# MLP with block products by seven in a hybrid decoder layer: operand sums moved to VectorE, splits spread over the group, weight sums issued earlier, last group as eight plain products

## The chip, the core and the metric

The kernel runs on one core of a Trainium2 chip. Its engines are TensorE (PE, matrix products, with PEld for loading the stationary operand), VectorE (DVE), ScalarE (ACT), GpSimd (POOL) and SyncE (SP, which only issues DMAs). Each engine works through its own queue in order; they wait for each other through semaphores. The metric is device time in microseconds (us), the median of several runs. The span of a profile is the time from its first to its last instruction; the time of that execution is a little longer.

## The reference

One decoder layer over 512 positions, width 1024, in float32: two attention branches merged by gates, an output projection, then an MLP with hidden width 4096 and squared ReLU, and a last RMSNorm. The change touches the MLP and the last norm alone:

```
h2 = rmsnorm(x, mlp_norm_g[l])
x = x + jnp.square(jax.nn.relu(h2 @ w_ff1[l])) @ w_ff2[l]
...
return rmsnorm(x, final_norm_g)
```

## The kernel before

Float32 products are made of three float32r products: each operand is split into a high part (ACT copies it to float32r, `hi`) and a low part (DVE subtracts, `lo`), and `mm3` adds hi·hi, hi·lo and lo·hi in PSUM. A matmul has a stationary operand of 128x128 and up to 512 columns.

The MLP runs over 8 groups of 512 hidden channels. For a group, four ff1 blocks (`ff1`, called a, b, c, d here; 24 matmuls each) give z = relu(.)², held as z0 and z1 (two blocks of 128 channels each, 512 tokens). The product of z (512 tokens by 512 channels) with 512 rows of w_ff2 (by 1024 columns) is then made as a 2x2 block product with seven instead of eight block multiplications (Winograd's form of Strassen's algorithm). Its operands (`ORDER`) are A11, A12, A22 (blocks of z), the sums S1 to S4 of blocks of z, B11, B21, B22 (blocks of w_ff2) and the sums T1 to T4 of blocks of w_ff2. A product k is a `pair` of two units (m = 0, 1), six matmuls of 512 columns each, 12 together, into PSUM tiles `pl` (four of them). Its result goes into `acc`, the residual of 512x1024, or into the running sums U (products 0 and 3) and V (product 2), all by DVE (L987 to L995).

- The sums S (`operand_a`) are POOL operations on 128x512; `put_a` then splits an A operand (ACT L959, DVE L960).
- `raw` loads a B block (512 KB, SP, L921). `tsum` makes a T: SP loads one block (L926) and POOL issues an accumulating DMA that adds the other (L927, from w_ff2 or from another T). There are three buffers for B blocks, three for T. `put_b` splits a B operand (ACT L967, DVE L968) into one of five buffers.
- The weights of ff1 come through `pre` (SP L112, ACT L119, DVE L121), two blocks ahead.
- `ff1` evicts its PSUM tile by ACT: relu (L911), then square (L912).

In group g the order is 0 a 1 2 b 3 4 c 5 d 6: digits are the products of group g, letters the ff1 blocks of group g+1. The order on PE is that of the code. On the other engines a scheduler sets the order when the program is built. Before, S1, S2, S4 and S3 of the next group and the splits of its operands 1 to 5 stand together behind block d. The last group has no ff1 blocks; it does the products 0 and 1, then 2 to 6 for m = 0 and for m = 1, and `finish` folds U and V into `acc` between them; `final` makes the last norm and stores rows of the result.

Of the kernel before, what the change touches and what calls it, by code (L numbers as in the profile page):

```python
# [10 lines left out]
F32 = mybir.dt.float32  # L11
F32R = mybir.dt.float32r
# [37 lines left out]
def body(nc, tc, ctx, a, out, dbg=lambda name, ap: None):  # L50
# [880 lines left out]
    def load(g, i):  # L931
        if g < NG:
            f, key = LOADS[i]
            f(g, key)

    def operand_a(g, key):
        z0, z1 = Z.get((g, 0)), Z.get((g, 1))
        t0, t1 = slice(0, 256), slice(256, 512)
        if key[0] == "A":
            return (z0, z1)[int(key[2]) - 1][:, :, (t0, t1)[int(key[1]) - 1]]  # L940
        if (g, key) not in SS:
            t = SS[g, key] = z_p.tile([128, 2, 256], F32, tag="s", name=key, bufs=3)
            if key == "S1":
                pool.tensor_tensor(t, z0[:, :, t1], z1[:, :, t1], op=ALU.subtract)
            elif key == "S2":
                pool.tensor_tensor(t, operand_a(g, "S1"), z0[:, :, t0], op=ALU.subtract)
            elif key == "S3":
                pool.tensor_tensor(t, z0[:, :, t0], z0[:, :, t1], op=ALU.subtract)
            else:
                pool.tensor_tensor(t, z1[:, :, t0], operand_a(g, "S2"), op=ALU.add)  # L950
        return SS[g, key]

    def put_a(g, k):
        if k % 2 == 0:
# [6 lines left out]
        AS[g, "op", k] = (hi, lo)  # L961

    def put_b(g, k):
        key = ORDER[k][1]
# [8 lines left out]
    def unit(g, k, m, cuts=(0, 512)):  # L973
        p = pl_tile()
        ah, al = AS[g, "op", k]
        bh, bl = BS[g, k]
        ms = slice(m * 128, (m + 1) * 128)
        for lo, hi in zip(cuts, cuts[1:]):
            c = slice(lo, hi)
            mm3(p[:, c], [(ah[:, q, ms], al[:, q, ms], bh[:, q, c], bl[:, q, c]) for q in range(2)])  # L980
            i, n = BLOCK.get(k, (0, 0))
            b = 2 * i + m
            cs = slice(512 * n + lo, 512 * n + hi)
            if k in BLOCK:
                t = acc[:, b, cs]
                if k == 5:
                    dve.tensor_tensor(t, t, p[:, c], op=ALU.subtract)  # L987
                else:
                    dve.tensor_tensor(t, p[:, c], t, op=ALU.add)  # L989
            t = {0: U, 2: V, 3: U}.get(k)  # L990
            if t is not None:
                if g == 0 and k != 3:
                    act.activation(t[:, m], p, AF.Copy)
                else:
                    dve.tensor_tensor(t[:, m], p[:, c], t[:, m], op=ALU.add)  # L995
            if g == NG - 1:
                finish(k, m, b, n, cs)

    def finish(k, m, b, n, cs):
        c12, c21, c22 = acc[:, m, 512:], acc[:, 2 + m, :512], acc[:, 2 + m, 512:]  # L1000
        if k == 3:
            pool.tensor_tensor(c21, c21, U[:, m], op=ALU.add)
            pool.tensor_tensor(V[:, m], U[:, m], V[:, m], op=ALU.subtract)
            pool.tensor_tensor(c12, c12, V[:, m], op=ALU.subtract)
        elif k == 5:
            pool.tensor_tensor(c21, c21, c22, op=ALU.subtract)
            dve.tensor_tensor(c22, c22, V[:, m], op=ALU.subtract)
        if k in (1, 4, 5, 6):
            final(b, n, cs)

    def pair(g, k):
        for m in range(2):
            unit(g, k, m)
        n = NP * g + k + NBS
        if n < NP * NG:
            put_b(*divmod(n, NP))

    def group(g):
        for step in "0a1 2b3 4c5 d6 ":
            if step.isdigit():  # L1020
                pair(g, int(step))
                load(g + 1, int(step))
            elif step != " ":
                ff1(4 * (g + 1) + "abcd".index(step))
            if step == "b":
                put_a(g + 1, 0)
            if step == "d":
                for k in range(1, 6):
                    put_a(g + 1, k)
        put_a(g + 1, 6)  # L1030

    def last_group(g):
        for k in range(2):
            pair(g, k)
        for m in range(2):
            for k in range(2, NP):
                unit(g, k, m, (0, 256, 512) if m and k == NP - 1 else (0, 512))
# [54 lines left out]
    for k in range(NP):  # L1092
        put_a(0, k)
        if k < NBS:
            put_b(0, k)
# [8 lines left out]
    last_group(NG - 1)  # L1104
    ff_st.close()
    right.close()

# [44 lines left out]
```

## Time and profile before

| | |
|---|---|
| median of the runs | 762.25 us |
| lowest | 758.26 us |
| the profiled execution | 762.06 us, span 760.3 us |
| PE busy | 701.6 us (92%) |
| DVE, ACT, POOL busy | 520.7, 366.1, 252.8 us (68%, 48%, 33%) |
| granted TensorE clock, mean | 0.963 of full speed |

Busy shares are means over stages with different limits; the group loop of the MLP runs from about 386 us to the end. The granted clock has two levels, full (2.4 GHz) and half (1.2 GHz); a mean between them in a stretch says that both occurred.

### The profile page before, as it was taken

Reading aid. Unit: us, or ns where it says so; the run is one execution under the profiler, and the core shown is the slowest. Engines: PE = TensorE matmul, PEld = TensorE weight load, DVE = VectorE, ACT = ScalarE, POOL = GpSimd, SP = SyncE. Lnnn points to the kernel's source line nnn. Section 1 sums busy time; section 2 is a strip of 40 time slices with the busy share of each in tenths; the row PEclk is TensorE's granted clock in tenths of the full one; section 3 lists DMA queues with packets and bytes.
Section 4 is the critical chain, followed back from the end, with each engine's and each line's share of the span. In section 5 each row is a group of like instructions: output and inputs, shape, how many; then the busy total and the mean of one; then the engine's idle time right before and its main releaser. Section 6 shows DMA issues by size and latency. Waiting matters only on the chain.

```text
span 760.3 us, 10231 instructions
## 1 busy us (share of the span) xinstructions
PE 701.6 (92%) x3653; PEld 563.8 (74%) x3654; DVE 520.7 (68%) x920; ACT 366.1 (48%) x631; POOL 252.8 (33%) x275
## 2 busy tenths in 40 slices
PE   8999999999999999999975989989899897999962
PEld 7879787778657778888954877868788686877852
DVE  6587899999998646833337558385664947557483
ACT  6566866646444456511426444344534534444333
POOL 2323677742365413200214141130413104141265
PEclk9999999999999999999996999989999998999996
DMA  8532521122311178800486956658476584644303
GB/s 316 194 119 81 159 87 43 56 70 87 109 42 44 56 273 318 254 27 1 154 238 178 254 145 185 175 139 210 122 212 176 140 214 131 180 111 108 87 1 110
DMA packets 43235, 106.55 MB, mean 140 GB/s; under 512 B 4464, under 2 KB 5360, under 8 KB 43184
## 3 DMA queue, kind: packets, MB, share of 16 engines
q1 hardware_dynamic: 35664, 88.04, 34.7%
q0 software_dynamic: 6656, 16.78, 12.7%
q10 hardware_dynamic: 864, 1.08, 0.4%
q8 instruction: 29, 0.48, 0.3%
q14 instruction: 22, 0.18, 0.1%
HBM read 90.28 MB, written 6.29 MB: 127 GB/s over the span
## 4 chain that ended last, share of the span: by engine, by line
PE 50%; DVE 18%; DMA 17%; POOL 5%; ACT 5%; issue 4%; SPq 0%; POOLq 0%; DVEq 0%; ACTq 0%
DMA T<-wff 8%; DMA T<-T 7%; PE pl L141 6%; PE pl L143 6%; PE pl L142 6%; PE pl L237 3%; PE pl L238 3%; PE pl L239 3%; DVE b L968 3%; PE pt L141 2%; PE pt L142 2%; PE pt L143 2%; DVE nmx L590 2%; DVE oh L714 2%; DVE as L960 2%
## 5 line engine op out<-in xcount | busy, mean ns | idle before, releaser
L141 PE MATMUL pl<-b,as 128*128 128x512 f32 (+1 forms) x226 | 94.7, 419 | 42.5 <-ACT z L911 18.2
L121 DVE TENSOR_TENSOR wlo<-wraw,whi 128x1024 fp32r<-128x1024 f32 (+1 forms) x60 | 73.8, 1231 | 68.5 <-ACT whi L119 67.7
L119 ACT ACTIVATE whi<-wraw 128x1024 fp32r<-128x1024 f32 (+1 forms) x71 | 74.5, 1049 | 87.5 <-PE pt L142 69.7
L143 PE MATMUL pl<-b,as 128*128 128x512 f32 (+1 forms) x226 | 93.2, 412 | 1.9 <-DVE as L960 1.9
L142 PE MATMUL pl<-b,as 128*128 128x512 f32 (+1 forms) x226 | 93.2, 412 | 0.0
L141 PE MATMUL pt<-h2h,whi 128*128 128x512 f32 x232 | 90.3, 389 | 0.0
L142 PE MATMUL pt<-h2l,whi 128*128 128x512 f32 x232 | 90.3, 389 | 0.0
L143 PE MATMUL pt<-h2h,wlo 128*128 128x512 f32 x232 | 90.3, 389 | 0.0
L141 PEld LDWEIGHTS pl<-b,as 128*128 128x128 f32 x226 | 46.0, 203 | 56.0 <-ACT z L911 20.6
L927 POOL DMA_DIRECT2D T<-wff x16 | 19.6, 1239 | 129.5 <-DMA T<-wff 60.8
L927 POOL DMA_DIRECT2D T<-T x16 | 14.1, 880 | 129.2 <-DMA T<-wff 60.3
L968 DVE TENSOR_TENSOR b<-T,b 128x1024 fp32r<-128x1024 f32 x32 | 39.7, 1240 | 24.6 <-ACT b L967 24.6
L143 PEld LDWEIGHTS pl<-b,as 128*128 128x128 f32 x226 | 46.0, 203 | 12.6 <-DVE as L960 2.7
L960 DVE TENSOR_TENSOR as<-S,as 128x512 fp32r<-128x512 f32 x32 | 33.4, 1081 | 29.7 <-ACT as L959 29.5
L142 PEld LDWEIGHTS pl<-b,as 128*128 128x128 f32 x226 | 46.1, 204 | 9.5
L967 ACT ACTIVATE b<-T 128x1024 fp32r<-128x1024 f32 x32 | 33.6, 1052 | 37.7 <-DMA T<-T 15.6
L141 PEld LDWEIGHTS pt<-h2h,whi 128*128 128x128 f32 x232 | 43.8, 189 | 9.2
L142 PEld LDWEIGHTS pt<-h2l,whi 128*128 128x128 f32 x232 | 43.6, 188 | 9.2
L143 PEld LDWEIGHTS pt<-h2h,wlo 128*128 128x128 f32 x232 | 43.6, 188 | 9.1
L714 DVE TENSOR_SCALAR oh<-posbc,thr 128x400 bf16<-128x400 f32 (+31 forms) x128 | 45.7, 410 | 3.8 <-PE pl L735 3.6
L989 DVE TENSOR_TENSOR acc<-pl,acc 128x512 f32<-128x512 f32 (+1 forms) x65 | 42.4, 671 | 7.8 <-PE pl L143 4.5
L595 POOL TENSOR_SCALAR pra<-pra,rs 128x400 f32<-128x400 f32 (+31 forms) x32 | 35.2, 1110 | 35.1 <-DVE rs L594 35.0
(315 smaller groups left out, 1730.6 us busy)
## 6 DMA issues: line engine op xcount, KB each, us to landing
wraw<-wff SPq DMA_DIRECT2D x32, 512.0 KB, 4.5
T<-wff SPq DMA_DIRECT2D x32, 512.0 KB, 4.5
wraw<-wF SPq DMA_DIRECT2D x24, 512.0 KB, 3.3
B<-wff SPq DMA_DIRECT2D x24, 512.0 KB, 6.4
T<-wff POOLq DMA_DIRECT2D x16, 512.0 KB, 7.6
T<-T POOLq DMA_DIRECT2D x16, 512.0 KB, 5.0
gd<-gt SPq DMA_DIRECT2D x16, 256.0 KB, 2.2
wraw<-wbr SPq DMA_DIRECT2D x8, 512.0 KB, 4.4
```

The lines of the kernel that those rows point to most:

```text
L119: act.activation(hi, raw, AF.Copy)
L121: eng.tensor_tensor(lo, raw, hi.bitcast(F32), op=ALU.subtract)
L141: pe.matmul(ps, lh, rh, start=(i == 0), stop=False)
L142: pe.matmul(ps, lh, rl, start=False, stop=False)
L143: pe.matmul(ps, ll, rh, start=False, stop=(i == n - 1))
L595: pool.tensor_scalar(pr, pr, rs, None, op0=ALU.mult)
L714: dve.tensor_scalar(oh[:, :n], posbc[:, :n], thr[:, 4 * G + q:4 * G + q + 1], None, op0=ALU.is_le)
L927: pool.dma_start(t, TT[g, y] if y[0] == "T" else wsrc(g, y), accum_op=ALU.add)
L960: dve.tensor_tensor(lo, x, hi.bitcast(F32), op=ALU.subtract)
L967: act.activation(t[:, 0], x, AF.Copy)
L968: dve.tensor_tensor(t[:, 1], x, t[:, 0].bitcast(F32), op=ALU.subtract)
L989: dve.tensor_tensor(t, p[:, c], t, op=ALU.add)
```

## The change

The operand sums S1 to S4 become DVE operations, in a function `asum`, and are issued at given places of the group. S1 and S2 of the next group come after block d, S3 and the split of A12 after product 6; the splits of products 2 to 6 come in their own group (after products 0, 1, 2 and so on). The T sums T1, T3, T2 of the next group are all issued after product 1, T4 after product 4; the B splits keep their places but go through a list `bq`. The last group is made of eight plain block products: its two halves of z are split whole (`last_put`, 128x1024), U and V are folded into `acc` before it (`last_sums`), and each block of 128x512 of the result gets 12 matmuls, one eviction and `final`. PE's order in groups 0 to 6 doesn't change.

```
-    LOADS = ((raw, "B11"), (raw, "B21"), (tsum, "T1"), (tsum, "T3"), (tsum, "T2"), (raw, "B22"), (tsum, "T4"))
...
+    def asum(g, key):
+        z0, z1 = Z[g, 0], Z[g, 1]
+        t0, t1 = slice(0, 256), slice(256, 512)
+        x, y, op = {"S1": (z0[:, :, t1], z1[:, :, t1], ALU.subtract),
+                    "S2": (SS.get((g, "S1")), z0[:, :, t0], ALU.subtract),
+                    "S3": (z0[:, :, t0], z0[:, :, t1], ALU.subtract),
+                    "S4": (z1[:, :, t0], SS.get((g, "S2")), ALU.add)}[key]
+        t = SS[g, key] = z_p.tile([128, 2, 256], F32, tag="s", name=key, bufs=3)
+        dve.tensor_tensor(t, x, y, op=op)
...
-                pool.tensor_tensor(t, z0[:, :, t1], z1[:, :, t1], op=ALU.subtract)
...
-            if g == NG - 1:
-                finish(k, m, b, n, cs)
...
+    LASTB = ("B11", "B21", "B12", "B22")
+
+    def last_put(j):
+        t = utile(j, F32R, "al")
+        hi, lo = t[:, 0:2], t[:, 2:4]
+        act.activation(hi, Z[NG - 1, j], AF.Copy)
+        dve.tensor_tensor(lo, Z[NG - 1, j], hi.bitcast(F32), op=ALU.subtract)
+        AS[j] = (hi, lo)
+
+    def last_sums():
+        for m in range(2):
+            uv = V[:, m]
+            dve.tensor_tensor(uv, U[:, m], uv, op=ALU.subtract)
+            c12, c21, c22 = acc[:, m, 512:], acc[:, 2 + m, :512], acc[:, 2 + m, 512:]
+            pool.tensor_tensor(c12, c12, uv, op=ALU.subtract)
+            dve.tensor_tensor(U[:, m], U[:, m], c22, op=ALU.subtract)
             pool.tensor_tensor(c21, c21, U[:, m], op=ALU.add)
...
+            dve.tensor_tensor(c22, c22, uv, op=ALU.subtract)
+
+    def last_group():
+        g = NG - 1
+        for b in range(NB):
+            ms = slice(b * 128, (b + 1) * 128)
+            cuts = (0, 512, 768, 1024) if b == NB - 1 else (0, 512, 1024)
+            for lo, hi in zip(cuts, cuts[1:]):
+                n, cs = lo // 512, slice(lo, hi)
+                c = slice(lo - 512 * n, hi - 512 * n)
+                p = pl_tile()[:, c]
+                mm3(p, [(AS[j][0][:, q, ms], AS[j][1][:, q, ms], BS[g, 2 * n + j][0][:, q, c],
+                         BS[g, 2 * n + j][1][:, q, c]) for j in range(2) for q in range(2)])
+                dve.tensor_tensor(acc[:, b, cs], p, acc[:, b, cs], op=ALU.add)
+                final(b, n, cs)
...
     def group(g):
-        for step in "0a1 2b3 4c5 d6 ":
-            if step.isdigit():
-                pair(g, int(step))
-                load(g + 1, int(step))
-            elif step != " ":
-                ff1(4 * (g + 1) + "abcd".index(step))
-            if step == "b":
-                put_a(g + 1, 0)
-            if step == "d":
-                for k in range(1, 6):
-                    put_a(g + 1, k)
-        put_a(g + 1, 6)
...
+        pair(g, 0)
+        for key in ("B11", "B21", "B12" if plain else "B22"):
+            raw(nxt, key)
+        put_a(g, 2)
+        asum(g, "S4")
+        ff1(4 * nxt)
...
+        pair(g, 1)
+        nb()
+        if not plain:
+            for key in ("T1", "T3", "T2"):
+                tsum(nxt, key)
+        put_a(g, 3)
+        pair(g, 2)
+        nb()
+        put_a(g, 4)
+        ff1(4 * nxt + 1)
...
+        put_a(g, 5)
+        pair(g, 3)
+        nb()
+        put_a(g, 6)
+        pair(g, 4)
+        nb()
...
+            tsum(nxt, "T4")
+        ff1(4 * nxt + 2)
...
+        pair(g, 5)
+        nb()
+        ff1(4 * nxt + 3)
+        if not plain:
+            asum(nxt, "S1")
+            asum(nxt, "S2")
+        pair(g, 6)
+        nb()
+        if plain:
+            last_put(1)
+            last_sums()
+        else:
+            asum(nxt, "S3")
+            put_a(nxt, 1)
...
-    for i in range(NP):
-        load(0, i)
+    for key in ("B11", "B21", "B22"):
+        raw(0, key)
+    for key in ("T1", "T3", "T2"):
+        tsum(0, key)
```

How the program's order changes is shown at three places; the numbers behind names tell one buffer from another.

DVE around the change from group 1 to group 2, from the splits of A12 (`z1`) and S1 on, before (`acc` and `U` from `pl` are evictions; the first `U` is that of product 0, unit 0):

```order
L960 TENSOR_TENSOR as_5167<-z1_5245,as_5167 128x512
L960 TENSOR_TENSOR as_5304<-S1_5305,as_5304 128x512
L989 TENSOR_TENSOR acc_3754<-pl_5330,acc_3754 128x512
L968 TENSOR_TENSOR b_5338<-B22_5267,b_5338 128x1024
L960 TENSOR_TENSOR as_5304<-S2_5309,as_5304 128x512
L960 TENSOR_TENSOR as_5313<-S4_5314,as_5313 128x512
L960 TENSOR_TENSOR as_5313<-S3_5318,as_5313 128x512
L960 TENSOR_TENSOR as_5344<-z1_5245,as_5344 128x512
L989 TENSOR_TENSOR acc_3754<-pl_5347,acc_3754 128x512
L995 TENSOR_TENSOR U_4606<-pl_5347,U_4606 128x512
```

The same place of DVE now:

```order
L937 TENSOR_TENSOR S1_5305<-z0_5079,z1_5250 128x512
L981 TENSOR_TENSOR acc_3754<-pl_5309,acc_3754 128x512
L937 TENSOR_TENSOR S2_5307<-S1_5305,z0_5079 128x512
L981 TENSOR_TENSOR acc_3754<-pl_5317,acc_3754 128x512
L960 TENSOR_TENSOR b_5325<-B22_5041,b_5325 128x1024
L937 TENSOR_TENSOR S3_5328<-z0_5079 128x512
L952 TENSOR_TENSOR as_5170<-z1_5250,as_5170 128x512
L981 TENSOR_TENSOR acc_3754<-pl_5332,acc_3754 128x512
L987 TENSOR_TENSOR U_4606<-pl_5332,U_4606 128x512
L981 TENSOR_TENSOR acc_3754<-pl_5341,acc_3754 128x512
L987 TENSOR_TENSOR U_4606<-pl_5341,U_4606 128x512
L952 TENSOR_TENSOR as_5356<-S1_5305,as_5356 128x512
```

The sums S1 and S2 stand on DVE ahead of the evictions of product 6, the split of S1 stands behind the evictions of product 0 instead of ahead of them, and the splits of S4, S3 and A22 have left this place.

POOL in groups 1 and 2 before (DMA rows are accumulating transfers into a T):

```order
L927 DMA T1_4818<-wff2 128x2x512
L927 DMA T3_4876<-wff2 128x2x512
L927 DMA T2_4898<-T3_4876 128x1024
L927 DMA T4_5028<-T2_4898 128x1024
L927 DMA T1_5131<-wff2 128x2x512
L944 TENSOR_TENSOR S1_4992<-z0_4775,z1_4932 128x512
L946 TENSOR_TENSOR S2_4996<-S1_4992,z0_4775 128x512
L950 TENSOR_TENSOR S4_5001<-z1_4932,S2_4996 128x512
L948 TENSOR_TENSOR S3_5005<-z0_4775 128x512
L927 DMA T3_5189<-wff2 128x2x512
L927 DMA T2_5211<-T3_5189 128x1024
L927 DMA T4_5341<-T2_5211 128x1024
```

POOL now:

```order
L927 DMA T1_4791<-wff2 128x2x512
L927 DMA T3_4794<-wff2 128x2x512
L927 DMA T2_4797<-T3_4794 128x1024
L927 DMA T4_4903<-T2_4797 128x1024
L927 DMA T1_5104<-wff2 128x2x512
L927 DMA T3_5107<-wff2 128x2x512
L927 DMA T2_5110<-T3_5107 128x1024
L927 DMA T4_5216<-T2_5110 128x1024
```

Between the accumulating transfers of one group and the next no sum is left on POOL.

ACT at the start of the group loop, from the first split of T1 on, before:

```order
L967 ACTIVATE b_4696<-T1_4613 128x1024
L119 ACTIVATE whi_4746<-wraw_4744 128x1024
L911 ACTIVATE z1_4632<-pt_4653 128x512
L967 ACTIVATE b_4703<-T2_4619 128x1024
L912 ACTIVATE z1_4632<-z1_4632 128x512
L967 ACTIVATE b_4711<-B22_4622 128x1024
L959 ACTIVATE as_4680<-z1_4632 128x512
L959 ACTIVATE as_4718<-z1_4632 128x512
```

and now:

```order
L959 ACTIVATE b_4694<-T1_4615 128x1024
L119 ACTIVATE whi_4731<-wraw_4729 128x1024
L911 ACTIVATE z1_4632<-pt_4653 128x512
L912 ACTIVATE z1_4632<-z1_4632 128x512
L959 ACTIVATE b_4763<-T2_4621 128x1024
L951 ACTIVATE as_4629<-z1_4632 128x512
L951 ACTIVATE as_4724<-S1_4686 128x512
L985 ACTIVATE U_4606<-pl_4700 128x512
```

The split of T2 stands ahead of that of A12 (`as` from `z1`) in both; the square of z1 and the split of B22 have changed sides.

## Rows read from the trace of the kernel before

**Rows 1.** The waits, of PE alone: who was waited for, us in total, times, the longest.

```profile
PE pl L141 <- ACT z L911: 18.2, 6, 3.9
PE pl L141 <- ACT as L959: 11.0, 1, 11.0
PE pl L141 <- DVE acc L989: 8.5, 2, 6.7
PE pl L141 <- DVE U L995: 4.7, 1, 4.7
```

**Rows 2.** Busy time of each engine by stretches: us from the span's start, length, then busy us (and instructions) of PE, PEld, DVE, ACT, POOL, the granted clock, the DMA share and GB/s. The first is one whole group, from one product 2 to the next, the second the twelve matmuls behind the stop at its start.

```profile
503.71:549.67 45.96, 43.55 (x180) 35.49 (x181) 29.19 (x35) 19.89 (x27) 10.65 (x8) 0.94 0.65 172
503.70:509.20 5.50, 5.49 (x13) 4.31 (x14) 5.50 (x7) 1.50 (x3) 0.00 (x0) 0.52 0.32 105
```

**Rows 3.** The timeline of PE: start, us, instruction, and in brackets the idle time before it and what ended it. The first is a block d's first matmul, the second the first of product 6 behind it (24 matmuls later); then the first of a product 2 and of the block b behind it (12 later).

```profile
472.58 0.39 PE L141 MATMUL pt<-h2h,whi 128*128 128x512 f32 x1
...
478.02 0.39 PE L141 MATMUL pl<-b,as 128*128 128x512 f32 x1
...
503.71 0.76 PE L141 MATMUL pl<-b,as 128*128 128x512 f32 x1 [3.76 <-ACT z L911]
...
508.96 0.40 PE L141 MATMUL pt<-h2h,whi 128*128 128x512 f32 x1
```

**Rows 4.** The timeline of POOL around the same stop: the accumulating DMA, S1 and S3.

```profile
492.16 1.21 POOL L927 DMA_DIRECT2D T<-wff  x1 [8.15 <-DMA T<-wff]
492.91 1.79 POOL L944 TENSOR_TENSOR S<-z,z 128x512 f32<-128x512 f32 x1
...
497.73 2.28 POOL L948 TENSOR_TENSOR S<-z 128x512 f32<-128x512 f32 x1
```

**Rows 5.** The timeline of ACT: a weight split behind a block, the last square of z1, the split of S1, and the relu of the next block a.

```profile
478.00 1.06 ACT L119 ACTIVATE whi<-wraw 128x1024 fp32r<-128x1024 f32 x1 [4.15 <-PE pt L142]
...
487.73 0.63 ACT L912 ACTIVATE z<-z 128x512 f32<-128x512 f32 x1
...
494.73 0.63 ACT L959 ACTIVATE as<-S 128x512 fp32r<-128x512 f32 x1 [5.69 <-POOL S L944]
...
502.99 0.58 ACT L911 ACTIVATE z<-pt 128x512 f32<-128x512 f32 x1
```

**Rows 6.** The timeline of DVE: the splits of A12, S1 and three more sums, and the first U update.

```profile
489.06 0.69 DVE L960 TENSOR_TENSOR as<-z,as 128x512 fp32r<-128x512 f32 x1
495.39 1.23 DVE L960 TENSOR_TENSOR as<-S,as 128x512 fp32r<-128x512 f32 x1 [5.63 <-ACT as L959]
...
498.78 2.98 DVE L960 TENSOR_TENSOR as<-S,as 128x512 fp32r<-128x512 f32 x3
...
502.89 0.67 DVE L995 TENSOR_TENSOR U<-pl,U 128x512 f32<-128x512 f32 x1
```

**Rows 7.** Groups of DVE instructions by line and shape over the period 457.27 to 503.71: count, busy us, mean ns, idle time before.

```profile
L968 DVE TENSOR_TENSOR b<-T,b 128x1024 fp32r<-128x1024 f32 x4 | 4.9, 1218 | 1.4 <-ACT b L967 1.4
L960 DVE TENSOR_TENSOR as<-S,as 128x512 fp32r<-128x512 f32 x4 | 4.2, 1091 | 5.6 <-ACT as L959 5.6
...
L960 DVE TENSOR_TENSOR as<-z,as 128x512 fp32r<-128x512 f32 x3 | 2.1, 688 | 0.0
```

**Rows 8.** The same view over 401 to 412, in the first group, while POOL makes its sums there.

```profile
L960 DVE TENSOR_TENSOR as<-z,as 128x512 fp32r<-128x512 f32 x2 | 3.4, 1750 | 0.0
...
L968 DVE TENSOR_TENSOR b<-B,b 128x1024 fp32r<-128x1024 f32 x1 | 2.0, 1973 | 0.2 <-ACT b L967 0.2
```

**Rows 9.** The timeline of ACT in the first group: the split of T2.

```profile
402.04 1.06 ACT L967 ACTIVATE b<-T 128x1024 fp32r<-128x1024 f32 x1 [10.25 <-DMA T<-T]
```

**Rows 10.** The timeline of PE in the first group: product 1's first and third matmul, and the first of block b.

```profile
405.13 0.79 PE L141 MATMUL pl<-b,as 128*128 128x512 f32 x1 [11.02 <-ACT as L959]
...
408.29 0.79 PE L143 MATMUL pl<-b,as 128*128 128x512 f32 x1 [1.94 <-DVE as L960]
...
415.82 0.39 PE L141 MATMUL pt<-h2h,whi 128*128 128x512 f32 x1
```

**Rows 11.** The timeline of PE at the end: the first matmul of product 6 of group 6 (behind the last ff1 block), the last group's longest stops, and the last matmul.

```profile
714.72 0.39 PE L141 MATMUL pl<-b,as 128*128 128x512 f32 x1
...
728.02 0.77 PE L141 MATMUL pl<-b,as 128*128 128x512 f32 x1 [4.73 <-DVE U L995]
...
751.34 0.58 PE L141 MATMUL pl<-b,as 128*128 128x256 f32 x1 [6.74 <-DVE acc L989]
...
752.58 0.41 PE L143 MATMUL pl<-b,as 128*128 128x256 f32 x1
```

**Rows 12.** The timeline of DVE at the end: a sum of `finish`, and the last eviction.

```profile
738.48 1.75 DVE L1007 TENSOR_TENSOR acc<-acc,V 128x512 f32<-128x512 f32 x1 [2.72 <-POOL acc L1006]
...
753.85 0.42 DVE L989 TENSOR_TENSOR acc<-pl,acc 128x256 f32<-128x256 f32 x1
```

**Rows 13.** The timeline of ACT at the end: the square of the last ff1 block, behind the relu and the gain row.

```profile
716.67 0.61 ACT L912 ACTIVATE z<-z 128x512 f32<-128x512 f32 x1
```

**Rows 14.** Line L927, the accumulating DMAs: the issuing instruction (ns min/median/max, first and last start), and the us from issue to landing.

```profile
L927 POOL DMA_DIRECT2D T<-wff x16: 1199/1208/1464, 379.4 to 692.1; - x16
...
DMA to landing us min/median/max: 4.5/6.3/11.2
```

**Rows 15.** Line L926, the plain loads of a T: us from issue to landing.

```profile
DMA to landing us min/median/max: 3.5/4.5/7.7
```

More of the change, by code (lines that the diff above doesn't have):

```diff
@@ L927, in tsum @@
         pool.dma_start(t, TT[g, y] if y[0] == "T" else wsrc(g, y), accum_op=ALU.add)
-    LOADS = ((raw, "B11"), (raw, "B21"), (tsum, "T1"), (tsum, "T3"), (tsum, "T2"), (raw, "B22"), (tsum, "T4"))
[L931 to L934, printed above, removed]
-    def operand_a(g, key):
[L937 to L943, printed above, removed]
-                pool.tensor_tensor(t, z0[:, :, t1], z1[:, :, t1], op=ALU.subtract)
[L945 to L951, printed above, removed]
+    def asum(g, key):
[7 more added lines that the diff above has]
+        dve.tensor_tensor(t, x, y, op=op)
+    def operand_a(g, key):
+        if key[0] == "S":
+            return SS[g, key]
+        i, j = int(key[1]) - 1, int(key[2]) - 1
+        return Z[g, j][:, :, 256 * i:256 * i + 256]
     def put_a(g, k):
@@ L963, in put_b @@
     def put_b(g, k):
-        key = ORDER[k][1]
+        key = ORDER[k][1] if g < NG - 1 else LASTB[k]
         x = (RAW if key[0] == "B" else TT)[g, key]
@@ L995, in unit @@
                     dve.tensor_tensor(t[:, m], p[:, c], t[:, m], op=ALU.add)
-            if g == NG - 1:
-                finish(k, m, b, n, cs)
-    def finish(k, m, b, n, cs):
-        c12, c21, c22 = acc[:, m, 512:], acc[:, 2 + m, :512], acc[:, 2 + m, 512:]
-        if k == 3:
-            pool.tensor_tensor(c21, c21, U[:, m], op=ALU.add)
[L1003 to L1009, printed above, removed]
+    LASTB = ("B11", "B21", "B12", "B22")
[12 more added lines that the diff above has]
+            dve.tensor_tensor(U[:, m], U[:, m], c22, op=ALU.subtract)
+            pool.tensor_tensor(c21, c21, U[:, m], op=ALU.add)
+            dve.tensor_tensor(c22, c22, uv, op=ALU.subtract)
[12 more added lines that the diff above has]
+                final(b, n, cs)
     def pair(g, k):
@@ L1013, in pair, with nb @@
             unit(g, k, m)
-        n = NP * g + k + NBS
-        if n < NP * NG:
-            put_b(*divmod(n, NP))
     def group(g):
-        for step in "0a1 2b3 4c5 d6 ":
-            if step.isdigit():
-                pair(g, int(step))
-                load(g + 1, int(step))
-            elif step != " ":
-                ff1(4 * (g + 1) + "abcd".index(step))
-            if step == "b":
-                put_a(g + 1, 0)
-            if step == "d":
-                for k in range(1, 6):
-                    put_a(g + 1, k)
-        put_a(g + 1, 6)
[L1032 to L1037, printed above, removed]
+        nxt = g + 1
+        plain = nxt == NG - 1
+        def nb():
+            if bq:
+                put_b(*bq.pop(0))
+        pair(g, 0)
[4 more added lines that the diff above has]
+        ff1(4 * nxt)
+        if g == 0:
+            nb()
[12 more added lines that the diff above has]
+        if not plain:
+            put_a(nxt, 0)
+        put_a(g, 5)
[3 more added lines that the diff above has]
+        pair(g, 4)
+        nb()
+        if plain:
+            raw(nxt, "B22")
+        else:
+            tsum(nxt, "T4")
+        ff1(4 * nxt + 2)
+        if plain:
+            last_put(0)
+        pair(g, 5)
+        nb()
+        ff1(4 * nxt + 3)
+        if not plain:
+            asum(nxt, "S1")
+            asum(nxt, "S2")
+        pair(g, 6)
+        nb()
+        if plain:
+            last_put(1)
+            last_sums()
+        else:
+            asum(nxt, "S3")
+            put_a(nxt, 1)
     parts = {b: 0 for b in range(NB)}
@@ L1087, in body @@
     pool.tensor_tensor(acc[:, 2:4, :512], acc[:, 2:4, :512], acc[:, 2:4, 512:], op=ALU.add)
-    for i in range(NP):
-        load(0, i)
+    for key in ("B11", "B21", "B22"):
+        raw(0, key)
+    for key in ("T1", "T3", "T2"):
+        tsum(0, key)
+    bq = [(g, k) for g in range(NG) for k in range(NP if g < NG - 1 else 4)]
     for j in range(4):
         ff1(j, p0[j] if j < 3 else None)
[L1092 to L1095, printed above, removed]
+        if j == 1:
+            put_a(0, 0)
+    put_b(*bq.pop(0))
+    put_b(*bq.pop(0))
+    for i in range(3):
+        asum(0, f"S{i + 1}")
+    put_a(0, 1)
+    put_b(*bq.pop(0))
+    tsum(0, "T4")
     for g in range(NG - 1):
@@ L1103, in body @@
     act.activation(gf, gf, AF.Copy, scale=float(D) ** 0.5)
-    last_group(NG - 1)
+    last_group()
     ff_st.close()
```

## Prediction, made before the changed kernel ran

> **What bounds the kernel now.** I read the waits of PE first, then PE's own timeline, then the queues of the engines it waits for. PE is busy for nearly the whole span, so what can be won is the time in which it stands. Its long waits lie in the MLP's group loop and name few causes [rows 1]: six stops of 18.2 us together ("ACT z"), one of 11.0 in the first group, the rest in the last group.
>
> The six are one stop per group. At full speed 24 matmuls take 478.02 − 472.58 = 5.44 us, 0.2267 each; after the stop at 503.71 the twelve of product 2 take 5.25 [rows 3], 0.44 each, and the granted clock of that stretch is 0.52 [rows 2], the lower of its two levels (1.2 GHz). A group has 180 matmuls (seven products of 12, four ff1 blocks of 24), 40.8 us at full speed; it takes 45.96 [rows 2].
>
> The stop comes at product 2. That product takes over the PSUM tiles of product 0 (four tiles, two to a product), so it needs S1 split and product 0 evicted. Going back: POOL can compute S1 only after the accumulating DMA that stands ahead of it in its queue, which waited for a landing until 492.16; S1 starts at 492.91 [rows 4], though its operands were ready at 488.36. ACT idles 5.69 us for it, DVE 5.63 [rows 5, 6]. Then A's splits run one behind the other on DVE, slowly beside POOL's sums, and only behind them stand the evictions of product 0: the U update of 502.89 ends at 503.56, and PE starts at 503.71. The view names "ACT z L911" because that ends at the same moment (502.99 + 0.58 [rows 5]); product 2 doesn't read that z. So the chain is POOL's queue, S1, a burst on DVE, an eviction, PE.
>
> **The change, part by part.** Sums are made against the profiled execution: span 760.3, 762.06 us with what lies around it (1.8), within 0.2 of the median of 762.25.
>
> *Sums on DVE, splits spread.* Per group POOL loses four sums and DVE gains four. A DVE split of 128x512 takes 0.69 with no POOL sum about, 1.09 in the mean beside them [rows 7], 1.75 in the worst stretch [rows 8]. I take 0.69 for the new ones: in the group loop POOL then only issues DMAs. The critical point: let 0 be the end of ff1 block d. ACT first splits a weight (1.06, as at 478.00 [rows 5]), DVE follows with 1.22, and ACT evicts and squares z meanwhile, so S1 starts at +2.3. In DVE's new order the low half of S1 is the twelfth operation from there: eleven of 0.6 to 0.69 and one B split of 1.22, ending between +10.1 and +11.1. PE has products 6 and 0, block a and product 1 to do first, 60 matmuls, and wants it at +13.6: a slack of 2.5 to 3.5. A12 (the seventh, about +7.5) is wanted at +10.9. DVE's load is 29.19 us per group now [rows 2], plus 4 × 0.69, less the slow rows: about 31 of 40.8. So I count the six stops as gone whole: from block b of group 0 (415.82 [rows 10]) to product 6 of group 6 (714.72 [rows 11]) stand 1188 matmuls, 269.3 us at 0.2267, in 298.9 us. **−29.6 us**, stops and lower clock together.
>
> A split takes 0.69 where POOL is quiet and 1.23 and more beside a POOL sum [rows 6, 7]. The Trainium skill says why (SBUF — State Buffer, "Who interferes with whom"): a DVE instruction with two SBUF inputs contends with a GpSimd instruction that reads SBUF. By that rule nothing in the group loop contends any more, and 0.69 holds for every row; by the slow rows DVE would need some 52 us a group, which is the third rival.
>
> *Weight sums sooner.* The T sums are now issued when a buffer is free, with no sum of POOL's between. The latest is T2: T3's base waits for the split of the old T3, about +10 from a group's first product, and lands in 4.5 [rows 15]; then two accumulations at 1.2 + 6.3 [rows 14]: +29.5. ACT comes to its split after product 5, at +32.6. Nothing lost; with the longest landings (7.7, 11.2, 11.2) it would be +42.5, which is the first rival.
>
> *First group.* Here the stop stays. T2's split still stands ahead of A12's in ACT's queue, and T2 lands at 402.0 [rows 9]. That landing ends a DMA burst of the same transfers; B22 is now ahead of T1, T3 and T2. I put T2 0.7 us later (between −3 and +1.5). Behind it ACT now has A12 at once: 402.04 + 0.7 + 1.06 + 0.63 = 404.4 for product 1, instead of 405.13, and its low half isn't held up by POOL (now a second stop of 1.94 [rows 10]). Products 1 and 2, half of them at the lower clock, take 8.0, and 0.3 for A12's low half: block b starts at 412.7 instead of 415.82. **−3.1 us.**
>
> *Last group.* It has 96 matmuls for 84: 12 × 0.2267 = 2.7 us more, on the path. It drops the S chain once more (a stop of 4.73) and the sums through U and V between products, which end in a stop of 6.74 before the last six matmuls [rows 11], with DVE waiting up to 2.72 on POOL's additions [rows 12]. These sums now run during product 6 and the blocks before, beside PE. From the end of block d: z relu, the gain row (it lands as now), the square, then a split of 128x1024 on ACT and DVE: 716.67 + 0.61 [rows 13] + 1.06 + 1.22 = 719.6. Product 6 ends at 714.72 + 2.72 = 717.44; eight more matmuls need only what is ready earlier, until 719.2. A stop of 0.3 to 1; I take 0.6. Then 96 × 0.2267 = 21.8; a block of 2.72 us brings DVE an eviction and at most a scaling and ACT a square and at most a scaling, each of the 128x512 size (0.6 to 0.7), so neither falls behind. The end behind the last matmul is the same chain, 760.3 − 752.99 = 7.3, in which DVE comes to its last eviction only at 753.85 [rows 11, 12]; I take 7.0. From product 6's end: 0.6 + 21.8 + 7.0 = 29.4, instead of 760.3 − 717.44 = 42.9. **−13.5 us.**
>
> Sum: 760.3 − 29.6 − 3.1 − 13.5 = 714.1; with 1.8 around it, **716 us**.
>
> **The rivals.** *A smaller stop stays in each group.* S1's low half has 2.5 to 3.5 us of slack behind a strict row of operations. If each took 1.09, or if T2's split, which stands ahead of S1 on DVE, came at +42.5, S1 would be late by 2 to 3 us beyond the slack. Such a stop cost between its length and 2.6 more at the lower clock. Six times 1.5 to 4: 725 to 740 us. For it: nothing on DVE can overtake, and ACT waited 10.25 for one landing [rows 9]. Against: that landing stands in the first group's burst, and POOL is quiet.
>
> *The last group keeps its stops*, since folded sums, evictions and scalings meet on DVE: the 13.5 go, 729.
>
> *DVE becomes the bound, and the kernel slower.* Eleven splits and sums at 1.75, eleven weight splits at 1.97 [rows 8], sixteen evictions at 0.67: 51.7 us a group against 46.0. Six groups lose 34, less 3.1 and 13.5: 778 span, 780 us. It decides from 48.7 us a group. For it: those durations occur. Against: DVE is busy 29.19 of 45.96 now, and they occur only beside POOL's sums. The Trainium skill (Perfetto Trace Analysis, "Optimizing Scalar/DVE Operations") advises to offload DVE, even to GPSIMD, when it is saturated; the change does the opposite. By that rule this rival would hold if DVE were saturated; at 64% the trace says it isn't.
>
> *It doesn't do what it says:* the new load order delays T2 in the first group by one more landing, 7.7 [rows 15]: 724.
>
> **How the numbers follow.** Forecast 0.70 (709 to 724: T2's landing −3 to +1.5, up to 1 us in each group, the end ±1.5); small stops 0.16; last group 0.06; first group later 0.03; DVE the bound 0.02; something unseen 0.03. The range 708 to 733 takes the first, third and fourth case whole and half of the second, some 0.85. About 2% (747 to 777) is what a measurement of this kernel can tell from no change. Faster by more than that 0.93, within it 0.05, slower 0.02.
>
> **What the profile after would show.** Right: no stop of PE over 1 us between block b of group 0 and the end of group 6; a period of 40.8; splits near 0.69; PE standing about 10 us before product 1 of group 0; some 32 us from the last block d to the end. Wrong: a stop before product 2 of each group that ends with DVE; DVE busy 40 us a group; stops between the last group's blocks.

## The result, and the profile after the change

The changed kernel takes 713.3 us (median of four runs, 712.9 to 713.8), the kernel before 759.7 beside it (median of 758.3, 759.7 and 762.3): a ratio of 0.938, with a 95% interval of 0.935 to 0.942. A fourth run of the kernel before took 1767 us and is not counted here; it is one of the three behind the median of 762.25 given ahead of the prediction, which without it is 760.3. The profiled execution took 713.8 us with a span of 712.0. The forecast was 716 us, between 708 and 733.

PE's long waits, from the view that sums them by cause (in all, times, longest), against [rows 1]:

```profile
engine line waited for: us in total, times, longest us
PE pl L141 <- ACT as L951: 9.3, 1, 9.3
PE pa L160 <- DVE warmb L157: 1.1, 1, 1.1
```

One stop is left, that of the first group. The six of the groups and those of the last group are gone. Six stretches of one group each, from block b of group 0 on (columns: stretch, length, PE, PEld, DVE, ACT and POOL busy, granted clock, DMA share, GB/s), answer [rows 2]:

```profile
411.32:452.12 40.80, 40.80 (x182) 33.80 (x180) 30.84 (x39) 21.16 (x29) 5.87 (x6) 1.00 0.82 220
452.12:492.92 40.80, 40.80 (x182) 33.80 (x180) 29.50 (x39) 19.93 (x26) 4.73 (x5) 1.00 0.73 194
...
615.32:656.12 40.80, 40.80 (x182) 33.80 (x180) 29.51 (x39) 19.94 (x26) 2.30 (x3) 1.00 0.46 117
```

PE is busy all of it at full clock (granted clock 1.00), 40.80 for 180 matmuls instead of 45.96, and DVE's load is nearly what it was (29.5 against 29.2; about 31 was forecast): four sums of 0.69 more, and splits that no longer run slowly. By form in the second stretch, against [rows 7] (count, busy us, mean ns, idle before):

```profile
L960 DVE TENSOR_TENSOR b<-T,b 128x1024 fp32r<-128x1024 f32 x5 | 6.1, 1221 | 0.6 <-ACT b L959 0.6
L952 DVE TENSOR_TENSOR as<-S,as 128x512 fp32r<-128x512 f32 x4 | 2.7, 683 | 0.0
L952 DVE TENSOR_TENSOR as<-z,as 128x512 fp32r<-128x512 f32 x3 | 2.1, 688 | 0.0
```

S1 on DVE, against [rows 4, 6] (start, length). The first row is S1, the second the eviction that held PE up before (the U update of unit 0 of product 0), the last the low half of S1:

```profile
478.81 0.69 DVE L937 TENSOR_TENSOR S<-z,z 128x512 f32<-128x512 f32 x1
...
484.16 0.68 DVE L987 TENSOR_TENSOR U<-pl,U 128x512 f32<-128x512 f32 x1
...
485.96 0.68 DVE L952 TENSOR_TENSOR as<-S,as 128x512 fp32r<-128x512 f32 x1
```

The spans of all kernels, cut at two rows of PE's timeline: the start of block b of group 0, and the start of product 6 of group 6, whose twelve matmuls take 2.72 (us; the loop between them has 1188 matmuls, 269.3 at full clock):

| kernel | block b | loop | behind product 6 | span |
|---|---|---|---|---|
| before | 415.8 | 298.9 | 42.9 | 760.3 |
| after | 411.3 | 269.3 | 28.7 | 712.0 |
| before, sums on DVE | 414.9 | 269.3 | 41.6 | 728.5 |
| before, new last group | 415.4 | 289.9 | 28.7 | 736.7 |
| before, both of these | 414.7 | 269.3 | 28.8 | 715.5 |
| after, sums on POOL | 411.0 | 269.3 | 30.0 | 713.0 |
| after, old loads | 410.5 | 269.3 | 28.8 | 711.3 |
| after, old last group | 410.1 | 269.3 | 47.2 | 729.3 |
| after, T2's high half on POOL | 400.7 | 274.7 | 28.7 | 706.8 |
| after, T2 on POOL | 400.7 | 281.4 | 28.7 | 713.5 |
| after, S1 made five times | 410.4 | 269.3 | 28.7 | 711.1 |
| after, S1 made eleven times | 410.8 | 310.9 | 28.8 | 753.2 |

### The profile page after: what moved, and what is told of

Its sections match the earlier page's. It is cut to its first block, busy times and chain, and to the rows that moved or that the text cites. A ratio compares the mean times of both kernels' runs of the same rounds, so it can differ in the third digit from the quotient of the medians.

```text
span 712.0 us, 10174 instructions
## 1 busy us (share of the span) xinstructions
PE 690.6 (97%) x3672; PEld 559.1 (79%) x3672; DVE 511.1 (72%) x936; ACT 362.3 (51%) x623; POOL 187.6 (26%) x235
## 4 chain that ended last, share of the span: by engine, by line
PE 79%; DVE 12%; DMA 4%; issue 2%; ACT 1%; POOL 1%; SPq 0%; POOLq 0%; DVEq 0%; ACTq 0%
PE pl L141 10%; PE pl L143 10%; PE pl L142 10%; PE pt L141 7%; PE pt L143 7%; PE pt L142 7%; PE pl L237 3%; PE pl L238 3%; PE pl L239 3%; DVE nmx L590 2%; DVE oh L714 2%; PE pl L845 2%; PE pl L844 2%; PE pl L846 2%; DVE sc L401 2%
## 5 line engine op out<-in xcount | busy, mean ns | idle before, releaser
L141 PE MATMUL pl<-b,as 128*128 128x512 f32 x196 | 77.4, 395 | 9.3 <-ACT as L951 9.3
L142 PE MATMUL pl<-b,as 128*128 128x512 f32 x196 | 77.2, 394 | 0.0
L143 PE MATMUL pl<-b,as 128*128 128x512 f32 x196 | 77.1, 393 | 0.0
L141 PEld LDWEIGHTS pl<-b,as 128*128 128x128 f32 x196 | 37.4, 191 | 17.4 <-ACT as L951 9.7
L927 POOL DMA_DIRECT2D T<-wff x14 | 17.2, 1243 | 115.6 <-DMA T<-wff 39.0
L959 ACT ACTIVATE b<-T 128x1024 fp32r<-128x1024 f32 x28 | 29.8, 1063 | 33.1 <-PE pl L143 15.8
L237 PE MATMUL pl<-hh,whi 128*128 128x512 f32 x112 | 44.7, 399 | 0.0
L927 POOL DMA_DIRECT2D T<-T x14 | 12.3, 880 | 121.4 <-DVE U L987 41.9
L239 PE MATMUL pl<-hh,wlo 128*128 128x512 f32 x112 | 43.7, 390 | 0.0
L143 PEld LDWEIGHTS pl<-b,as 128*128 128x128 f32 x196 | 37.3, 190 | 8.1 <-DVE as L952 0.2
L238 PE MATMUL pl<-hl,whi 128*128 128x512 f32 x112 | 43.7, 390 | 0.0
L142 PEld LDWEIGHTS pl<-b,as 128*128 128x128 f32 x196 | 37.4, 191 | 7.8
```

The lines of the kernel that those rows point to most:

```text
L141: pe.matmul(ps, lh, rh, start=(i == 0), stop=False)
L142: pe.matmul(ps, lh, rl, start=False, stop=False)
L143: pe.matmul(ps, ll, rh, start=False, stop=(i == n - 1))
L237: pe.matmul(p, h[:, k], hh[k], start=(k == 0), stop=False)
L238: pe.matmul(p, h[:, k], hl[k], start=False, stop=False)
L239: pe.matmul(p, l[:, k], hh[k], start=False, stop=(k == NK - 1))
```

## Experiments

**The sums alone.** In the kernel before, S1 to S4 change engine, nothing else:

```
-                pool.tensor_tensor(t, z0[:, :, t1], z1[:, :, t1], op=ALU.subtract)
+                dve.tensor_tensor(t, z0[:, :, t1], z1[:, :, t1], op=ALU.subtract)
...
```

> The kernel before with one edit: S1 to S4 are made by DVE instead of POOL; their place in the code, the burst of splits behind block d, the loads and the last group stay. Theory (the stop of each group comes from S1 standing in POOL's queue behind an accumulating DMA): S1 starts 2 to 4 us behind block d's end instead of 14.9, the burst of eight operations of 0.69 us is over before product 0 has to be evicted, and the six stops of about 5 us go whole: periods near 41, some 29 us less, 729 to 736 us (S1 no longer late in the last group either). Rival (the burst itself, standing ahead of the evictions, makes the stop): DVE has four operations more in the burst, the period stays 44 to 46, 750 to 762 us. Second rival (DVE's load): splits no faster than now, 760 us or more.

Measured: 729.7 us, ratio 0.962 (0.957 to 0.967). All six stops are gone, with the burst still there. ACT's weight split behind block d, then on DVE S1, a split of the burst, and the update of U that ends it:

```profile
480.15 1.06 ACT L119 ACTIVATE whi<-wraw 128x1024 fp32r<-128x1024 f32 x1 [4.15 <-PE pt L142]
482.40 0.69 DVE L944 TENSOR_TENSOR S<-z,z 128x512 f32<-128x512 f32 x1
...
487.89 0.68 DVE L960 TENSOR_TENSOR as<-S,as 128x512 fp32r<-128x512 f32 x1
...
491.42 0.68 DVE L995 TENSOR_TENSOR U<-pl,U 128x512 f32<-128x512 f32 x1
```

From S1's start to the end of that update pass 9.7 us, against 10.65 before (492.91 to 503.56 [rows 4, 6]). S1 comes 2.25 us behind the start of ACT's weight split instead of 6.75, so that U is updated 5.45 us sooner: 4.5 of it are the start of S1, 0.95 the burst. The rows of the kernel before behind the 6.75, ACT's weight split and PE's first matmul behind block d:

```profile
486.16 1.06 ACT L119 ACTIVATE whi<-wraw 128x1024 fp32r<-128x1024 f32 x1 [3.36 <-PE pt L142]
486.19 0.39 PE L141 MATMUL pl<-b,as 128*128 128x512 f32 x1
```

The first two matmuls of [rows 3], at 472.58 and 478.02, are named wrongly there: they begin a block c and product 5. Block d follows at 480.75, and product 6 begins at 486.19. So S1 came 6.7 us behind block d's end, not the 14.9 of the expectation, and the sums on DVE take 4.5 us off that, not 11 to 13. The forecast doesn't rest on these names: it takes from the rows only the pace of 0.2267.

**The new places alone, sums on POOL.** In the changed kernel:

```
-        dve.tensor_tensor(t, x, y, op=op)
+        pool.tensor_tensor(t, x, y, op=op)
```

> The changed kernel with S1 to S4 made by POOL again, at their new places; spread splits, loads and last group as changed. Theory (what counts is when S1 is there and that no burst stands ahead of the evictions): POOL comes to S1 behind one accumulating DMA, which in the changed kernel it issues 4.5 us behind block d's end, so S1 is ready at about +7, its low half at +8 to +11, and PE wants it at +13.6: no stop or one under 1 us, 713 to 720 us. Rival (contention: DVE's splits are slow beside POOL's sums, and this made the stops): splits of 1.0 to 1.7 us through the row of operations, S1's low half 2 to 4 us late in each group, 728 to 742 us. Rival (the engine alone, POOL's queue at any place): the six stops come back, 738 to 745 us.

Measured: 715.3 us, ratio 0.943 (0.939 to 0.948); no stop in any group, one of 1.4 us in the last. ACT's weight split behind block d, POOL (the issue of an accumulating DMA, S1, and the last of the four sums) and DVE:

```profile
476.26 1.06 ACT L119 ACTIVATE whi<-wraw 128x1024 fp32r<-128x1024 f32 x1 [3.78 <-PE pt L142]
481.27 1.21 POOL L927 DMA_DIRECT2D T<-wff  x1 [7.88 <-DMA T<-wff]
482.02 1.79 POOL L937 TENSOR_TENSOR S<-z,z 128x512 f32<-128x512 f32 x1
...
486.84 2.28 POOL L937 TENSOR_TENSOR S<-z,S 128x512 f32<-128x512 f32 x1
...
484.51 1.22 DVE L952 TENSOR_TENSOR as<-S,as 128x512 fp32r<-128x512 f32 x1 [4.05 <-ACT as L951]
485.65 2.31 DVE L960 TENSOR_TENSOR b<-B,b 128x1024 fp32r<-128x1024 f32 x1
487.88 0.68 DVE L981 TENSOR_TENSOR acc<-pl,acc 128x512 f32<-128x512 f32 x1
488.49 0.67 DVE L987 TENSOR_TENSOR U<-pl,U 128x512 f32<-128x512 f32 x1
```

S1 again stands behind the accumulating DMA: ACT's weight split behind block d starts at 476.26, S1 at 482.02, 5.8 us later (before 6.75, so S1 is only 1.0 sooner here). DVE stood 4.05 us, and a B split took 2.31 instead of 1.22. But only two splits stand between S1 and the evictions now, not six, and U is updated at 489.16, before PE takes its tile at 489.88. So either edit removes the stops: the stop needed a late S1 and a burst ahead of the evictions. The slow rows beside POOL's sums are those with two operands in SBUF; the evictions, with one in PSUM, kept 0.68, though POOL's sum of 486.84 runs beside them. That is what the Trainium skill states (SBUF — State Buffer, "Who interferes with whom"): a DVE instruction with at most one SBUF input, outside the 2-port perf modes, doesn't contend with GpSimd.

**The loads.** The groups' loads of weight blocks and the T sums return to one behind each product:

```
-            for key in ("T1", "T3", "T2"):
-                tsum(nxt, key)
+            raw(nxt, "B21")
...
+            tsum(nxt, "T1")
```

> The changed kernel with the loads of a group's weight blocks and the T sums back at their old places in the code (one behind each product), for all groups but the first and the last. Theory (a T sum starts when its buffer comes free, and the place in the code doesn't set that): no difference, 712 to 715 us, period 40.8. Rival (the earlier T sums are part of the gain): T2's split comes late and holds S1 up behind it on DVE, stops of 1 to 3 us in each group, 720 to 732 us.

Measured: 713.0 us (712.9 to 713.5), period 40.80. The place in the code sets nothing here: SP's queue has the same order of loads in this kernel and in the changed one, ACT and DVE have the same rows in the same order, and the kernel before differs from both on SP only up to group 1 and in the last group. A load of a T sum's base waits for its buffer, and SP's waits there end with a split on DVE or with the accumulating transfer that reads the old T. So this run shows that the edit moved no load; what a T sum issued sooner would be worth, no run shows.

**The last group, twice.** First the old one in the changed kernel, its splits spread as in the other groups:

> The changed kernel with the last group as before: seven products, U and V folded in between them; its operand sums and splits are made as in the other groups (DVE sums, spread). Theory (the last group's gain of 13 to 14 us is made of its stop for the S operands of 4.7, the lower clock behind it, the stop for the sums through U and V of 6.7, and the waits of DVE on POOL, less 2.7 us for 12 more matmuls): spreading removes the first, so about half comes back: 718 to 722 us. Rival (the eight products give the whole of it, the S chain being late in the last group however the sums are made): 725 to 728 us. Rival (the fold alone costs nothing beside the products): 711 to 714 us.

Measured: 732.2 us, 19 more than the changed kernel; no theory gave that. Behind product 6 stand 47.2 us, more than in the kernel before itself. PE's largest stops by the view of its waits, and from DVE's timeline its waits for POOL's folding of U and V (L1015):

```profile
PE pl L141 <- DVE ss L1110: 10.5, 1, 10.5
...
PE pl L143 <- DVE as L952: 5.8, 2, 4.8
```

```profile
702.77 0.69 DVE L981 TENSOR_TENSOR acc<-pl,acc 128x512 f32<-128x512 f32 x1 [4.07 <-POOL acc L1015]
...
715.14 0.69 DVE L981 TENSOR_TENSOR acc<-pl,acc 128x512 f32<-128x512 f32 x1 [3.94 <-POOL acc L1015]
```

The view's "ss" is not what PE needs in the longest stop: DVE's last eviction ahead of it ends at the same moment (721.03), and it stands behind DVE's wait of 3.94. The chain DVE, POOL, DVE, PE runs twice, for m = 0 and for m = 1, and the spread splits, with no ff1 blocks between the products, come later than the burst did. So this is no clean undoing of the one part. The clean one is the new last group put into the kernel before:

> The kernel before with the new last group alone: eight plain products, U and V folded into the residual ahead of them; sums on POOL, burst of splits and loads of groups 0 to 6 as before. Theory (the last group's 42.9 us from product 6's end become 28.7, as in the changed kernel, whatever the other groups do): 13 to 14.5 us less than before, ratio about 0.982; of the long stops the six of the groups stay. Rival (part of that gain belongs to the sums on DVE, since the last group's S chain was the late one): 6 to 9 us less, ratio 0.989 to 0.992.

Measured: 739.1 us, ratio 0.975 (0.970 to 0.980): 19.0 us less. Behind product 6 stand 28.7 us, the 14.2 expected; most of the rest lies in the loop, 9.0 us shorter between the two profiled executions. Of these, 3.7 are group 6, which has no stop now (before: 1.95, and 1.7 at the lower clock behind it); 5.3 are the other groups, whose five stops stay and cost less in this execution. On POOL, S1 of group 5 and then of group 6, with all that stands between them:

```profile
624.21 1.21 POOL L927 DMA_DIRECT2D T<-wff  x1 [8.11 <-DMA T<-wff]
624.95 1.79 POOL L944 TENSOR_TENSOR S<-z,z 128x512 f32<-128x512 f32 x1
...
642.12 1.21 POOL L927 DMA_DIRECT2D T<-wff  x1 [10.07 <-DVE V L995]
651.28 0.90 POOL L927 DMA_DIRECT2D T<-T  x1 [7.96 <-DMA T<-wff]
659.79 0.86 POOL L927 DMA_DIRECT2D T<-T  x1 [7.60 <-DMA T<-wff]
666.77 1.29 POOL L944 TENSOR_TENSOR S<-z,z 128x512 f32<-128x512 f32 x1 [6.12 <-ACT z L912]
```

The plain last group has no T sums, so no accumulating DMA stands ahead of group 6's S1: it waits for z alone (ACT), not for a landing. On DVE, in group 6, the same burst, as slow as ever:

```profile
672.48 2.98 DVE L960 TENSOR_TENSOR as<-S,as 128x512 fp32r<-128x512 f32 x3
...
676.58 0.67 DVE L995 TENSOR_TENSOR U<-pl,U 128x512 f32<-128x512 f32 x1
```

PE goes on without a stop at 678.04, while in group 5 it stood 2.76 us. From S1's start to the end of the update of U pass 10.5 us, against 10.65 before. Same engine, same burst, same contention; only the wait in POOL's queue is missing. That shows the first link of the chain by itself.

**Two parts of four.** Sums on DVE and the new last group in the kernel before:

> The kernel before with two edits: S1 to S4 on DVE, and the new last group. The burst of splits behind block d, the loads and T sums, and the first group's code stay as before. It asks whether spreading the splits and issuing the T sums sooner add anything. Theory (they don't, outside the first group): the one-edit kernel with DVE's sums has a span of 728.5 with 41.6 us behind product 6's end, the new last group takes 28.7, so 715.6 span, about 717 us; the changed kernel's 713.3 is less by the 3.6 us by which its first group reaches block b sooner. Rival (the spread carries part of the gain once the last group is short, since its splits come behind the burst): 720 to 728 us.

Measured: 717.3 us (717.0 to 717.5). Spreading the splits and the new places of the T sums add nothing but 3.4 us at the start of the first group, whose own code this kernel also keeps as before; which of these gives the 3.4 no run shows.

**The slack of S1.** In the changed kernel S1 is made several times over, in groups 1 to 6; five times first:

```
-        dve.tensor_tensor(t, x, y, op=op)
+        for _ in range(5 if key == "S1" and g else 1):
+            dve.tensor_tensor(t, x, y, op=op)
```

> The changed kernel with S1 made five times over in the same tile, one after the other on DVE, in groups 1 to 7: four operations of 0.60 us spacing more ahead of S1's low half, 2.4 us. It measures the slack that the prediction gave S1 (2.5 to 3.5 us; the changed kernel's trace has 3.5). Theory: the low half is ready at +12.4 to +13.1 behind block d's end, PE's third matmul of product 2 wants it at +14.1: no stop, 713 to 715 us, period 40.8. Rival (the slack is smaller, since hi waits too or DVE's row slips): a stop of 0.5 to 2 us in each group, 717 to 730 us.

Measured: 713.7 us (712.8 to 713.9). The low half ends 12.4 us behind block d's end, and nothing stops. Then eleven times:

> The changed kernel with S1 made eleven times over on DVE in groups 1 to 6: ten operations of 0.60 us spacing more, 6.0 us, against a slack of 3.5. S1's low half becomes about the twenty-fourth operation behind block d, ready at +18 to +19, and PE wants it at +14.1. Theory (past the slack each us of DVE's row is a us of PE, and the lower clock costs 0 to 2.6 more at each stop): stops of 4 to 5 us in six groups, 738 to 757 us. Rival (the row of operations shifts into idle time further on and PE's order gives it room): under 730 us.

Measured: 755.7 us (753.4 to 756.8), nearly the time before the change. PE's stop at product 2 of one group, the matmul behind it, and the next (start, length, idle before):

```profile
499.62 0.80 PE L141 MATMUL pl<-b,as 128*128 128x512 f32 x1 [2.94 <-ACT as L952]
500.21 0.63 PE L142 MATMUL pl<-b,as 128*128 128x512 f32 x1
501.36 0.79 PE L143 MATMUL pl<-b,as 128*128 128x512 f32 x1 [0.52 <-DVE as L953]
...
547.32 0.72 PE L141 MATMUL pl<-b,as 128*128 128x512 f32 x1 [2.94 <-ACT as L952]
```

The period is 547.32 − 499.62 = 47.7, 6.9 over 40.8: 3.5 of waiting, and 3.4 because PE runs at the lower level through product 2 and into block b (a matmul each 0.43 instead of 0.2267; the granted clock from 499.62 to 505.00 is 0.50). The ten operations put S1's low half back by 8.2 us, to +18.2, since the scheduler puts a split of a T sum and two evictions ahead of it besides; what PE waits for is S1 itself, and no longer an eviction. So S1's low half 2.4 us later costs nothing, and 8.2 later 42 us in all.

**The first group.** POOL copies T2's high half in group 0, so that ACT's queue doesn't stand before T2's landing:

```
-        act.activation(t[:, 0], x, AF.Copy)
+        if (g, k) == (0, 3):
+            pool.tensor_copy(t[:, 0], x)
+        else:
+            act.activation(t[:, 0], x, AF.Copy)
```

> The changed kernel with one edit for group 0 alone: the high half of T2 is copied by POOL instead of ACT, so that ACT doesn't stand before T2's landing with the split of A12 behind it. T2's low half stays on DVE, ahead of product 1's evictions there. Theory (the first group's stop of 9.3 us is ACT's queue, not the data of product 1): product 1 starts at 394 to 396 instead of 403.4, products 1, 2 and block b end by 407; product 3 then waits for T2 (landing 401.7, a copy of 2 to 2.5 on POOL, 1.2 on DVE, two evictions) until 408 to 410.5, against 416.8 now: 6 to 9 us less, 704 to 707 us. Rival (the landings of the DMA burst hold product 2's or product 1's operands too): the stop moves to another operand at the same time, 711 to 714 us.

Measured: 708.4 us (707.6 to 708.8), ratio to the kernel before 0.934 (0.931 to 0.937): 4.9 less than the changed kernel and the fastest of all. PE at product 1 and at product 3:

```profile
393.74 0.50 PE L141 MATMUL pl<-b,as 128*128 128x512 f32 x1
...
395.57 0.50 PE L143 MATMUL pl<-b,as 128*128 128x512 f32 x1 [1.11 <-DVE as L952]
...
408.97 0.47 PE L141 MATMUL pl<-b,as 128*128 128x512 f32 x1 [2.66 <-DVE acc L984]
```

Product 1 starts 9.6 us sooner, and block b 10.6. Half is given back at product 3: its tile waits for evictions of product 1, which stand on DVE behind T2's low half, and the granted clock of the 7 us behind that stop is 0.76. The gain is a little under the 6 to 9 expected. With T2's low half on POOL too:

```
+            pool.tensor_tensor(t[:, 1], x, t[:, 0].bitcast(F32), op=ALU.subtract)
```

> As the kernel in which POOL copies T2's high half in group 0, with T2's low half on POOL too, so that nothing of T2 stands ahead of product 1's evictions on DVE. Theory: the evictions are done by about 401, T2's halves are ready at 404 and 406.5 behind its landing at 401.7, product 3 starts between 406.5 and 408: 8 to 10 us less than the changed kernel, 703 to 705 us, and 1 to 3 less than with the high half alone on POOL. Rival (POOL's two operations on 128x1024 take 3 us each or more, and DVE's splits slow down beside them): no better than the other, 705 to 709 us.

Measured: 714.5 us (713.7 to 715.2), worse than either theory. POOL in this kernel, then ACT's split of T4 and the two stops of PE:

```profile
402.58 1.37 POOL L960 CAST b<-T 128x1024 fp32r<-128x1024 f32 x1 [9.91 <-DMA T<-T]
404.04 2.39 POOL L961 TENSOR_TENSOR b<-T,b 128x1024 fp32r<-128x1024 f32 x1
406.38 0.86 POOL L927 DMA_DIRECT2D T<-T  x1
...
411.00 1.06 ACT L963 ACTIVATE b<-T 128x1024 fp32r<-128x1024 f32 x1 [10.82 <-DMA T<-T]
...
412.60 0.50 PE L141 MATMUL pl<-b,as 128*128 128x512 f32 x1 [3.33 <-ACT V L989]
...
445.78 0.80 PE L143 MATMUL pl<-b,as 128*128 128x512 f32 x1 [2.74 <-DVE as L952]
```

The product 3 that it was made for starts without a wait, at 406.10. But T4's accumulating DMA now stands behind 3.8 us of POOL's work and is issued at 406.38 (404.04 in the kernel above); ACT's split of T4 waits for its landing, and V's evictions of product 2 stand behind that split: PE stops 3.33 us later in product 3 instead. The delay goes on into group 1: its T2 lands at 437.5, ACT's split of it stood 7.75 us, and z, S1 and A12's low half stand behind it, so product 1 stops for 2.74. This is the first rival's mechanism (T2 late, S1 behind it), in a group where T2's margin had gone.

## Why the prediction was right, step by step

- **What bounds the kernel.** The chain (POOL's queue, S1, a burst on DVE, an eviction, PE) holds link by link: without POOL's wait, no stop (group 6 of the kernel before with the new last group); without the burst, none (sums on POOL at the new places). What the prediction did not say is that one link is enough, so that sums and spread splits, counted as one term, each give the whole of it.
- **Six stops, −29.6.** Exact: 298.9 to 269.3. S1 starts 2.24 behind the start of ACT's weight split (+2.3 said, 476.57 to 478.81), its low half is the twelfth operation and ends at 486.64, +10.0 (10.1 to 11.1 said). The slack, 2.5 to 3.5 against +13.6, was 3.6: a low half 2.4 us later stopped nothing, one 8.2 later stopped PE for 3.5.
- **Weight sums sooner, 0.** Right in the number, but not for the reason worked out: the order of the loads doesn't change in groups 2 to 6, so nothing was sooner there.
- **First group, −3.1.** It was 4.5. The term that was off is T2's landing, put 0.7 later: ACT's split of it starts 0.3 sooner. From kernel to kernel this stretch varies by as much: in the five other kernels with T2's split on ACT in this place, block b starts at 410.1 to 411.0 instead of 411.3. The stop now:

```profile
401.74 1.06 ACT L959 ACTIVATE b<-T 128x1024 fp32r<-128x1024 f32 x1 [9.21 <-DMA T<-T]
402.70 0.61 ACT L951 ACTIVATE as<-z 128x512 fp32r<-128x512 f32 x1
...
403.37 0.79 PE L141 MATMUL pl<-b,as 128*128 128x512 f32 x1 [9.27 <-ACT as L951]
```

  These are the rows that answer [rows 9, 10]: A12 directly behind T2 in ACT's queue, as said, and no second stop. Products 1 and 2 took 7.95 (8.0 and 0.3 said).
- **Last group, −13.5.** It was 14.2. The stop put at 0.6 was under 0.4: the ninth matmul, the first that needs the low half of the later z, starts 0.52 behind the eighth (684.90, 685.42). The matmuls took some 22.1 instead of 21.8, in part because the 24 of 256 columns take 0.12 each, more than half of 0.2267. What lies behind the last is 6.2 instead of 7.0: PE ends at 705.8, and DVE comes to its last eviction at once,

```profile
705.86 0.42 DVE L1020 TENSOR_TENSOR acc<-pl,acc 128x256 f32<-128x256 f32 x1 [0.27 <-PE pl L143]
```

  where before it was 0.9 us late [rows 11, 12]. The part is worth 14.2 by itself, as the kernel before with it alone shows; what it gives there beyond that, in group 6, whose S1 no longer waits, belongs to the six stops in the changed kernel.
- **Rivals.** Contention was real where POOL still made the sums (splits of 812 ns in the mean there, 683 without) and still made no stop. The price put on a small stop, its length and up to 2.6 for the lower clock, was too low: 3.5 us of waiting cost 6.9. DVE's load never became the bound: even with ten operations more it is busy 35.5 of 47.7 us, and what stops PE there is S1 late behind its row, the first rival's mechanism.

The sum came out 2.1 us too high in the span (714.1 against 712.0): 1.4 of it in the first group, 0.7 in the last.

## What to carry to other kernels

A short operation that others wait for should not stand in a queue behind one that waits for a transfer: read from the trace when its operands were ready and when it started. Where a stop needs two conditions, undo each alone before crediting a change that removes both; here two of four edits gave all but 3.4 us. And before an operation is moved into another queue, list what stands behind it there: one operation of 2.4 us on POOL, in one group of eight, put the issue of a DMA back by as much, and the kernel took 6 us longer.

## What the runs showed of the hardware

The clock does not follow the length of a stop alone. In the kernel before with the new last group, two stops read the same, and only behind the first did PE go on at its lower level (granted clock 0.50 from 546.74 to 549.80; 1.00 from 591.93 to 594.90):

```profile
546.74 0.76 PE L141 MATMUL pl<-b,as 128*128 128x512 f32 x1 [2.63 <-ACT z L911]
547.30 0.63 PE L142 MATMUL pl<-b,as 128*128 128x512 f32 x1
...
591.93 0.47 PE L141 MATMUL pl<-b,as 128*128 128x512 f32 x1 [2.63 <-ACT z L911]
592.24 0.40 PE L142 MATMUL pl<-b,as 128*128 128x512 f32 x1
```

Less the stop at its end, the period behind the first is 1.8 us over 40.8, that behind the second 0.3. In the kernel before, a stop of 2.99 (at 595.36) was followed by a granted clock of 1.00, one of 1.95 (at 685.80) by 0.59. What decides between the two stayed open; a price for a stop needs both ends. Kernels whose stops were gone also repeat more closely: the four runs of the changed kernel lie within 0.9 us, the four of the kernel before with the new last group, where five stops stay, between 736.9 and 741.8.
